# Storing half of group 10 of a linear-attention kernel in four DMAs of 96, 20, 10 and 2 partitions

One Trainium2 chip (trn2), one core. The metric is device time in microseconds (us); lower is better.

## The reference

```python
# Q, K, V: (8, 12, 512, 64) float32
Q_feat = np.maximum(0, Q) + 1
K_feat = np.maximum(0, K) + 1
KV = np.einsum('bhkd,bhkv->bhdv', K_feat, V)
K_sum = np.sum(K_feat, axis=2)
numerator = np.einsum('bhqd,bhdv->bhqv', Q_feat, KV)
denominator = np.einsum('bhqd,bhd->bhq', Q_feat, K_sum)
return (numerator / (denominator[:, :, :, None] + 1e-10)).astype(np.float32)
```

## The kernel before

The work goes through in 12 groups of 1 MB of output (`NG = 12`). The first load of K is issued by SyncE, in float32; the other loads cast to bf16 on their way and are issued by GpSimd, as are the stores of groups 0 to 9. The stores of groups 10 and 11 are issued by SyncE, each in two halves of 512 KB, so that a half can leave as soon as its multiplies on VectorE are done.

```python
    def view(t, c):
        return t.flatten_outer_dims().rearrange("(n p c) d -> p n c d", p=P, c=c)
    o_dram = view(out, C)                       # P = 128, C = 8, D = 64: 2 KB per (p, n)
    # ... cut ...
    def store(g):
        o_sb = outs.pop(g)                      # tile [128, 4, 8, 64] float32
        o_to = o_dram[:, g * NP : g * NP + NP]  # NP = 4
        if g < NG - 2:
            nc.gpsimd.dma_start(out=o_to, in_=o_sb)
            return
        for h in range(2):
            nc.sync.dma_start(out=o_to[:, h:NP:2], in_=o_sb[:, h:NP:2])
    # ... cut: features, transposes, matmuls ...
        # at the end of the program
        output(last - 1)                        # group 10
        output(last)                            # group 11
        for g in range(last - LAG, NG):         # groups 8, 9, 10, 11
            store(g)
```

A half store has 128 partitions with two runs of 2 KB each: 256 packets, 16 on each of 16 DMA engines.

Of the kernel before, what the change touches and what calls it, by code (L numbers as in the profile page):

```python
# [19 lines left out]
def kernel(  # L20
# [18 lines left out]
    nc = tc.nc  # L39

    B, H, S, D = Q.shape
    P = 128
# [3 lines left out]
    NP = 4  # L46
    NG = NPAIR // NP
# [64 lines left out]
    def store(g):  # L112
        o_sb = outs.pop(g)
        o_to = o_dram[:, g * NP : g * NP + NP]
        if g < NG - 2:
            nc.gpsimd.dma_start(out=o_to, in_=o_sb)  # L116
            return
        for h in range(2):
            nc.sync.dma_start(out=o_to[:, h:NP:2], in_=o_sb[:, h:NP:2])

    def feature(dst, src):
        nc.vector.tensor_scalar(  # L122
# [95 lines left out]
    with tc.manual_schedule():  # L218
# [15 lines left out]
        for g in range(NG - 1):  # L234
            k_features(g)
            v_blocks(g)
            q_features(g)
            if g:
                transposes(g - 1)
            if g >= 2:  # L240
                output(g - 2)
            keys_values(g)
            if g % 2 and g // 2 + 2 < NG // 2:
                load_pair(g // 2 + 2)
            if g >= LAG:
                store(g - LAG)
# [10 lines left out]
        for g in range(last - LAG, NG):  # L257
            store(g)
# [30 lines left out]
```

## Time and profile before

| | before |
|---|---|
| time, median of 3 (range) | 127.22 us (127.15 to 127.66) |
| span of the profiled run | 125.8 us |
| busy: DVE, ACT, PE, GpSimd | 70%, 54%, 52%, 22% |
| moved over the span | 400 GB/s |
| last semaphore increment of the last store | 124.87 us |

No engine of compute is near full; the DMA engines are, as the prediction shows below with the page's slices. Two more views matter. The first is the timeline of SyncE's queue (start, duration in us): its four stores.

```profile
115.35 0.38 SPq L119 DMA_DIRECT2D out_dram<-o_sb  x1
117.03 0.37 SPq L119 DMA_DIRECT2D out_dram<-o_sb  x1
118.71 0.37 SPq L119 DMA_DIRECT2D out_dram<-o_sb  x1
120.39 0.37 SPq L119 DMA_DIRECT2D out_dram<-o_sb  x1
```

The duration is the time that SyncE spends on issuing, not the transfer. The last one starts 0.03 us after the last multiply ends. The second view is the table of busy time by stretches (stretch, its length, busy time of PE, PEld, DVE, ACT, POOL with counts, granted clock, share of the 16 DMA engines, GB/s). Share and GB/s are to be read together: a low share is engines that have nothing to do, a high share with low GB/s is engines that are held up.

```profile
117.00:118.00 1.00, 0.52 (x12) 0.36 (x14) 0.93 (x5) 0.00 (x0) 0.00 (x0) 1.00 1.03 412
118.00:119.00 1.00, 0.58 (x16) 0.41 (x16) 0.96 (x3) 0.00 (x0) 0.00 (x0) 1.00 1.01 383
119.00:120.00 1.00, 0.16 (x6) 0.00 (x0) 0.97 (x3) 0.00 (x0) 0.00 (x0) 0.70 1.04 401
120.00:121.00 1.00, 0.00 (x0) 0.00 (x0) 0.36 (x1) 0.00 (x0) 0.00 (x0) 0.50 1.04 401
```

Before the change both are full: about 390 GB/s for each full share.

### The profile page before, as it was taken

What the parts mean: (1) busy time and instruction counts of PE and PEld (TensorE: products, weight loads), DVE (VectorE), ACT (ScalarE), POOL (GpSimd) and SP (SyncE); (2) the same over time, 40 slices, a digit from 0 to 9 for tenths busy, and PEclk for the clock granted to TensorE, in tenths of its full rate; (3) what the DMA queues carried; (4) which work ended last, traced back from release to release, by engine and by line L of the source; (5) the groups of instructions that cost most, each with busy time, mean ns of one, the idle gap of its engine ahead of it and who ended that gap; (6) DMA issues with size and microseconds to landing.
All of it is one profiled execution on the core that took longest, in us unless ns stands there. A gap on an engine that the chain in (4) does not pass through costs nothing.

```text
span 125.8 us, 2337 instructions
## 1 busy us (share of the span) xinstructions
PE 65.2 (52%) x960; PEld 48.4 (39%) x960; DVE 88.2 (70%) x188; ACT 68.0 (54%) x87; POOL 27.8 (22%) x43
## 2 busy tenths in 40 slices
PE   0005939000059784796918476006978569694500
PEld 0003627000036564574806365004656447472300
DVE  4896280206199799999989990629959999758920
ACT  7832296006700889629892962750087971987000
POOL 6990213000002082023700260212221002020000
PEclk9999999755555999689999999955589976999955
DMA  3999999999999999999999999999999999999991
GB/s 76 341 211 209 210 213 211 210 212 211 212 211 212 211 214 212 210 212 214 253 414 287 209 210 212 213 369 380 209 210 210 211 287 418 418 417 410 403 391 72
DMA packets 13419, 32.13 MB, mean 255 GB/s; under 512 B 608, under 2 KB 608, under 8 KB 13408
## 3 DMA queue, kind: packets, MB, share of 16 engines
q0 software_dynamic: 12048, 28.84, 98.3%
q1 hardware_dynamic: 1360, 3.15, 6.8%
q8 instruction: 7, 0.11, 0.3%
q14 instruction: 4, 0.03, 0.1%
HBM read 37.75 MB, written 12.58 MB: 400 GB/s over the span
## 4 chain that ended last, share of the span: by engine, by line
DMA 40%; DVE 26%; PE 18%; POOL 6%; issue 6%; DVEq 0%; POOLq 0%
DMA q_raw<-in_Q_dram 40%; DVE o_sb L200 15%; PE kva_ps L157 11%; DVE v_all L140 4%; PE qt_ps L176 3%; DVE recip L199 3%; PE o_ps L189 3%; POOL v_raw L99 2%; DVE qf L122 2%; DVE kf L122 2%; POOL q_raw L99 1%; POOL kva_diag L231 1%; POOL k_raw L99 1%; POOL identity masks.py:199 0%; POOL identity masks.py:197 0%
## 5 line engine op out<-in xcount | busy, mean ns | idle before, releaser
L157 PE MATMUL kva_ps<-v_all,kf 128*64 128x320 bf16 x384 | 36.4, 356 | 13.1 <-DVE v_all L140 13.1
L189 PE MATMUL o_ps<-kva_diag,qt 128*64 128x130 bf16 x384 | 19.1, 234 | 40.9 <-DVE o_sb L200 40.4
L200 DVE TENSOR_TENSOR o_sb<-o_ps,recip 128x512 f32<-128x512 f32 x48 | 33.2, 692 | 1.6
L140 DVE COPY v_all<-v_raw 32x2048 bf16<-32x2048 bf16 x36 | 26.5, 736 | 10.9 <-DMA v_raw<-in_V_dram 10.6
L157 PEld LDWEIGHTS <-kf 128*64 128x64 bf16 x384 | 25.3, 133 | 20.9 <-DVE v_all L140 13.3
L189 PEld LDWEIGHTS <-qt 128*64 128x64 bf16 x384 | 12.7, 114 | 46.4 <-DVE o_sb L200 44.6
L138 ACT COPY v_all<-v_raw 32x2048 bf16<-32x2048 bf16 x12 | 22.7, 1894 | 13.3 <-DMA v_raw<-in_V_dram 13.1
L177 ACT COPY qt<-qt_ps 128x1024 bf16<-128x1024 bf16 x24 | 29.7, 1308 | 0.3
L167 ACT CAST kva_diag<-kva_ps 64x256 bf16<-64x256 f32 x24 | 8.9, 371 | 33.3 <-PE kva_ps L157 33.2
L122 DVE TENSOR_SCALAR qf<-q_raw 128x1024 bf16<-128x1024 bf16 x24 | 9.1, 423 | 6.6 <-DMA q_raw<-in_Q_dram 6.5
L99 POOL DMA_DIRECT2D k_raw<-in_K_dram x7 | 5.3, 754 | 38.1 <-DVE kf L122 37.3
L116 POOL DMA_DIRECT2D out_dram<-o_sb x10 | 8.4, 846 | 22.6 <-DVE o_sb L200 16.4
L176 PE MATMUL qt_ps<-identity,qf 128*128 128x128 bf16 x192 | 13.1, 222 | 0.0
L199 DVE RECIPROCAL recip<-o_ps 128x8 f32<-128x8 f32 x48 | 9.6, 199 | 4.9 <-PE o_ps L189 4.8
L122 DVE TENSOR_SCALAR kf<-k_raw 128x1024 bf16<-128x1024 bf16 x22 | 8.7, 437 | 6.0 <-DMA k_raw<-in_K_dram 6.0
L176 PEld LDWEIGHTS <-qf 128*128 128x128 bf16 x192 | 11.0, 99 | 3.3 <-issue 3.0
L99 POOL DMA_DIRECT2D v_raw<-in_V_dram x8 | 6.1, 764 | 18.8 <-ACT v_all L138 10.7
L99 POOL DMA_DIRECT2D q_raw<-in_Q_dram x8 | 5.9, 741 | 4.2 <-DMA q_raw<-in_Q_dram 4.2
L213 DVE MEMSET v_all<- 128x3072 f32 (+1 forms) x2 | 4.4, 2192 | 1.1 <-DVE ones L225 0.7
L168 ACT CAST kva_diag<-kva_ps 64x4 bf16<-64x4 f32 x24 | 4.0, 169 | 0.0
L214 ACT COPY v_all<-zero 128x2048 f32<-128x2048 f32 x2 | 3.7, 1894 | 0.0
L214 ACT ACT_TABLE_LOAD x1 | 1.3, 1283 | 0.7 <-PEq L273 0.7
(12 smaller groups left out, 4.6 us busy)
## 6 DMA issues: line engine op xcount, KB each, us to landing
out_dram<-o_sb POOLq DMA_DIRECT2D x10, 1024.0 KB, 20.2
k_raw<-in_K_dram POOLq DMA_DIRECT2D x4, 1024.0 KB, 18.0
v_raw<-in_V_dram POOLq DMA_DIRECT2D x4, 1024.0 KB, 20.9
q_raw<-in_Q_dram POOLq DMA_DIRECT2D x4, 1024.0 KB, 25.0
v_raw<-in_V_dram POOLq DMA_DIRECT2D x4, 512.0 KB, 17.3
q_raw<-in_Q_dram POOLq DMA_DIRECT2D x4, 512.0 KB, 17.1
out_dram<-o_sb SPq DMA_DIRECT2D x4, 512.0 KB, 5.1
k_raw<-in_K_dram POOLq DMA_DIRECT2D x3, 512.0 KB, 23.3
```

Source lines behind the costliest of these rows:

```text
L99: nc.gpsimd.dma_start(out=t[:, ms], in_=drams[x][:, 2 * groups[0] : 2 * groups[-1] + 2])
L116: nc.gpsimd.dma_start(out=o_to, in_=o_sb)
L122: nc.vector.tensor_scalar(out=dst, in0=src, scalar1=1.0, scalar2=1.0, op0=ALU.add, op1=ALU.max)
L138: nc.scalar.copy(out=v_blk[g % 2][ps, b], in_=v_raw[ps])
L140: nc.vector.tensor_copy(out=v_blk[g % 2][ps, b], in_=v_raw[ps])
L157: nc.tensor.matmul(kva_ps[64 * n : 64 * n + 64], lhsT=kf[:, c, n, :], rhs=vb[:, :, n, c, :], start=(c == 0), stop=(c == C2 - 1),)
L167: nc.scalar.copy(out=kva[ps, :, n, 0:D], in_=kva_ps[ps, sb : sb + 4, :])
L176: nc.tensor.transpose(qt_ps[:, c, :], qf[:, half * C + c, :, :], identity)
L177: nc.scalar.copy(out=qt[:, :, :, half], in_=qt_ps)
L189: nc.tensor.matmul(ops[c // 4][64 * j : 64 * j + 64, c // 2 % 2, (c % 2) * W : (c % 2) * W + W], lhsT=qt[:, c, 32 * b : 32 * b + 32, :], r ...
L199: nc.vector.reciprocal(out=recip, in_=cells[:, :, :, :, D:D1])
L200: nc.vector.tensor_tensor(out=o_sb[:, h:NP:2, 4 * i : 4 * i + 4].rearrange("p n (b c) d -> p b c n d", b=2), in0=cells[:, :, :, :, 0:D], i ...
```

## The change

The DMA engines end one after another; some are late. By the section of the Trainium skill that the prediction cites first, a DMA from SyncE whose partitions don't divide by 16 runs on fewer engines, the lower-numbered ones. So the change cuts one half store in four, to move work from engines 10 to 15 to engines 0 to 9.

```diff
         for h in range(2):
-            nc.sync.dma_start(out=o_to[:, h:NP:2], in_=o_sb[:, h:NP:2])
+            parts = (0, 96, 116, 126, P) if (g, h) == (NG - 2, 0) else (0, P)
+            for lo, hi in zip(parts, parts[1:]):
+                nc.sync.dma_start(out=o_to[lo:hi, h:NP:2], in_=o_sb[lo:hi, h:NP:2])
```

## The prediction

> **What bounds the kernel now.** I read the page first: the slices, then the part on DMA issues, then the queue's own waits, and last the table by stretches of the end.
>
> ```profile
> DMA  3999999999999999999999999999999999999991
> GB/s 76 341 211 209 210 213 211 210 212 211 212 211 212 211 214 212 210 212 214 253 414 287 209 210 212 213 369 380 209 210 210 211 287 418 418 417 410 403 391 72
> ...
> out_dram<-o_sb POOLq DMA_DIRECT2D x10, 1024.0 KB, 20.2
> ...
> out_dram<-o_sb SPq DMA_DIRECT2D x4, 512.0 KB, 5.1
> ```
>
> The DMA engines are busy in every slice but the first and the last: the kernel is bound by its transfers from end to end. From the thirty-fourth slice on only stores run, at 391 to 418 GB/s until the last slice. The chain on the page ends in the last DVE multiply, but what ends the span is the landing of what that multiply released. The waits of SyncE's queue say so:
>
> ```profile
> SPq L119 <- DVE recip L199: 117.1, 3, 114.3
> SPq L284 <- DMA out_dram<-o_sb: 3.7, 3, 1.2
> ```
>
> Line 284 is the end of the program. Its 3.7 us in three waits are waits for the four stores of line 119 that SyncE issues, each 512 KB: group 10 half 0, group 10 half 1, group 11 half 0, group 11 half 1. The timeline of SyncE has them at 115.35, 117.03, 118.71 and 120.39 us, 0.37 us of issuing each and 1.68 us apart. The last multiply ends at 120.36, the span at 125.8. What moves between shows in the table of stretches (the last two columns are the mean share of the 16 DMA engines and GB/s):
>
> ```profile
> 120.50:121.00 0.50, 0.00 (x0) 0.00 (x0) 0.00 (x0) 0.00 (x0) 0.00 (x0) 0.50 1.02 393
> ...
> 122.00:122.50 0.50, 0.00 (x0) 0.00 (x0) 0.00 (x0) 0.00 (x0) 0.00 (x0) 0.50 1.03 401
> 122.50:123.00 0.50, 0.00 (x0) 0.00 (x0) 0.00 (x0) 0.00 (x0) 0.00 (x0) 0.50 0.78 303
> 123.00:123.50 0.50, 0.00 (x0) 0.00 (x0) 0.00 (x0) 0.00 (x0) 0.00 (x0) 0.50 0.43 164
> 123.50:124.00 0.50, 0.00 (x0) 0.00 (x0) 0.00 (x0) 0.00 (x0) 0.00 (x0) 0.50 0.17 66
> 124.00:124.50 0.50, 0.00 (x0) 0.00 (x0) 0.00 (x0) 0.00 (x0) 0.00 (x0) 0.50 0.06 25
> ```
>
> Up to 122.5 all engines work. Then the share goes 0.78, 0.43, 0.17, 0.06 (0.06 is one engine of 16): the engines run dry one after another, and the last works alone. If they ended together, the 0.5 x (0.78 + 0.43 + 0.17 + 0.06) = 0.72 us of full work left at 122.5 would be done by 123.2, and not at 124.5. So the most that any evening out of the engines can give is 1.3 us, one per cent of the time.
>
> The trace's record of the last store's semaphore gives this engine by engine. Its sixteen increments come at 122.98 us and, after that, at +0.02, 0.05, 0.07, 0.09, 0.16, 0.38, 0.54, 0.57, 0.60, 0.84, 0.88, 0.92, 1.31, 1.32 and 1.88 us, so the last at 124.87. Six stand apart, at +0.84 and later: ten engines are early and six late. From that last increment to the end of the span are 0.9 us of closing waits and drains, which the change leaves.
>
> The lag is older than this store: it is 2.3 to 2.5 us between the first and the last increment of every DMA from 90 us to 121 us, hardly growing while stores alone run. All engines then have the same work at the same rate; what was lost before is carried along, as no queue runs dry. Its origin can be seen early. In the DMA that landed first at 22.7 us the spread is 0.38 us. Next an instruction fetch of 16 KB starts at 23.1, and the DMA after it has fifteen increments within 0.35 us and one at 1.53.
>
> **What the Trainium skill says.** (1) The page DMA: Bandwidth & Descriptors, section Why a DMA increments its semaphore by 16 and not by 1: a DMA runs on the largest k of at most 16 engines that divides the slowest dimension of both sides, and from SyncE these are the lowest-numbered k. Hence 128 and 96 partitions take 16 engines, 20 and 10 take ten, 2 takes two. The trace agrees for 128 (sixteen spread increments per store); for the others nothing has run yet. (2) The same page, Latency and other measured facts: engines 7 and 15 are "usually slower" in traces. The trace here does not number the engines; it agrees that some are late, with one 0.56 us behind the rest. (3) Runtime: NRT & Kernel Launch, Instruction fetch mechanics: instruction memory is refilled in blocks of 16 KiB by DMA. The trace has seven such packets on the queue for instructions, and at least the one at 23.1 us left one engine 1.2 us late. (4) SBUF — State Buffer, Door 1: partitions 0 to 63 lie behind eight ports and 64 to 127 behind the other eight, so that a part of the partitions need not reach all sixteen. No row of the trace tests that; it feeds a rival below.
>
> **The change part by part.** It removes one store of 128 partitions and adds four of 96, 20, 10 and 2: the same bytes, so the sum of the work is unchanged.
> - Issue: four times 0.37 us is 1.49 us, from 115.35 to 116.84 with nothing between. The next store's data is there at 117.03, so 0.19 us is left for three gaps. Even a store issued 0.3 us late does no harm: the queued stores keep the engines busy (share 1.02 until 122.5).
> - Data: a partition has two runs of 2 KB, two packets. Before, each engine has 128/16 x 2 = 16. After: all engines get 96/16 x 2 = 12; the lowest ten get 2 x 2 = 4 more from the 20, and 1 x 2 = 2 from the 10; the lowest two get 2 from the last. That is 20 packets on engines 0 and 1, 18 on engines 2 to 9, 12 on engines 10 to 15 (40 + 144 + 72 = 256, as before).
> - A packet's time: the last packets of the trace, of the one engine still working, start at 123.976, 124.056, 124.136 and so on to 124.456 us, 80 ns apart. The 4 KB packets of the full stage start 155 to 156 ns apart on an engine, almost the same per byte. So an engine alone is no faster than one of sixteen, and an engine's end is its own count of packets times 80 ns. Engines 10 to 15 gain 4 x 80 = 0.32 us, engines 2 to 9 lose 0.16 us, engines 0 and 1 lose 0.32 us.
> - Completion packets: two or three more on the ten engines, 9 ns each: 0.02 to 0.03 us, none on the six.
> - The end: if the six late engines are the numbers 10 to 15, which the cut of ten to six fits, the last increment goes from +1.88 to +1.56, the next from +1.32 to +1.00; the early ten go at worst from +0.60 to +0.95. The slowest still decides, and all of its 0.32 us reach the end. If the second latest is among the ten, it goes to +1.50 and still does not decide. The early ones have slack besides: the records have the earliest engines dry for some 0.3 us before their part of the last store arrives.
> - Closing waits: three semaphores more, of DMAs long landed; each such wait took under 0.1 us and comes before the last. Nothing.
> Sum: 127.22 - 0.32 + 0 = 126.90 us.
>
> **The rivals.** (A) The late engine is not among 10 to 15. Engine 7 is one of the two that the skill names. Then the end goes up 0.16 us, or 0.32 if it is 0 or 1: 127.4 to 127.6 us. For it: no view here numbers the engines, and a fetch may fall to another engine in another execution. Against it: ten and six are just the split of the increments. (B) Ports: 96 partitions in runs of six put ten engines onto the even ports and six onto the odd ones, and the remainder then all reads behind odd ports. The engines that we want faster could wait. Against it: six engines have eight ports, and older stores are mixed in. If it takes half the gain: 127.05 us. (C) Issue: a store on fewer engines may take longer to issue than 0.37 us, or the four may wait on one another's landing (some 4.5 to 5 us from issue). The first costs nothing up to about a microsecond, because the late engine still has the older packets to do; the second would hold back the last store and give 129 us or more. The four write disjoint rows and read one tile, so I see no reason for it: 2%. (D) Nothing measurable: the three runs before span 127.15 to 127.66, 0.5 us, more than the effect.
>
> **Range and chances.** I give the step with 10 to 15 late seven or eight chances in ten (-0.32, or about half of it under B), and A two (+0.16 to +0.32). Weighted, that is about -0.2; the most likely is -0.3. I say 126.95 us. With the scatter of the runs, 0.2 us either way around either outcome, 126.55 to 127.45. Two per cent are 2.5 us: faster by that is impossible when evening out can give 1.3 us at most, so 0.01; slower needs C's second form, 0.01.
>
> **What would show it.** In the profile of the changed kernel: seven stores of line 119 on SyncE, the first four within 1.6 us from about 115.4; the last increment of the last store some 0.3 us earlier, with the sixteen spread by about 1.6 us and not 1.88; the share in the stretches after 122.5 higher at first and then gone by about 124.2; DVE, ACT and PE as before. An end at the old place or later with the latest increment at +2.0 or more would prove A; packets of over 100 ns in the first store's time on the late engine B; a late fourth store C.

## The result, and the profile after

The changed kernel takes 128.75 us in the median of 6 runs (128.43 to 129.48), the kernel before 127.38 beside it (127.15 to 127.98). The ratio is 1.011, with a 95% interval of 1.0069 to 1.0151. Ratios here are the mean time of one kernel's fast runs over that of the other's fast runs of the same rounds, so not quite the ratio of the medians quoted. It is 1.1% slower, within the two per cent of "same", but 1.8 us above the 126.95 predicted and outside the range.

The page's slices after the change:

```profile
DMA  3999999999999999999999999999999999999892
GB/s 89 331 212 208 212 210 212 210 208 212 212 211 213 212 215 210 211 213 215 274 417 259 207 213 211 221 400 343 212 210 213 210 337 423 417 413 413 265 368 107
```

In the place of 403 there is a slice at 265 GB/s. The table by stretches shows it in finer steps:

```profile
117.00:118.00 1.00, 0.58 (x12) 0.35 (x8) 0.97 (x3) 0.00 (x0) 0.00 (x0) 0.81 1.04 360
118.00:119.00 1.00, 0.12 (x4) 0.00 (x0) 0.97 (x3) 0.00 (x0) 0.00 (x0) 0.50 0.97 258
119.00:120.00 1.00, 0.00 (x0) 0.00 (x0) 0.15 (x1) 0.00 (x0) 0.00 (x0) 0.50 0.66 184
120.00:121.00 1.00, 0.00 (x0) 0.00 (x0) 0.00 (x0) 0.00 (x0) 0.00 (x0) 0.50 0.98 373
```

Both kinds of loss are there. From 118 to 119 the engines are busy (0.97) and move 258 GB/s, two thirds of what that share moved before: they are held up. From 119 to 120 the share falls to 0.66 as well: some have nothing to do. The timeline of SyncE's queue tells where the second comes from:

```profile
114.14 0.35 SPq L121 DMA_DIRECT2D out_dram<-o_sb  x1
114.54 1.34 SPq L121 DMA_DIRECT2D out_dram<-o_sb  x1
115.92 2.22 SPq L121 DMA_DIRECT2D out_dram<-o_sb  x1
118.18 0.26 SPq L121 DMA_DIRECT2D out_dram<-o_sb  x1
118.49 0.42 SPq L121 DMA_DIRECT2D out_dram<-o_sb  x1
118.96 2.01 SPq L121 DMA_DIRECT2D out_dram<-o_sb  x1
121.01 0.47 SPq L121 DMA_DIRECT2D out_dram<-o_sb  x1
```

The stores of 20 and 10 partitions took 1.34 and 2.22 us to issue, and a later one of 128 took 2.01. The last store was issued at 121.01 us, 1.86 us after its data was ready (the last multiply ended at 119.15; in this run the data came early), but only 0.62 us later than before (120.39).

The end, in half-microseconds, and the queue's last waits:

```profile
122.50:123.00 0.50, 0.00 (x0) 0.00 (x0) 0.00 (x0) 0.00 (x0) 0.00 (x0) 0.50 1.00 389
123.00:123.50 0.50, 0.00 (x0) 0.00 (x0) 0.00 (x0) 0.00 (x0) 0.00 (x0) 0.50 1.01 397
123.50:124.00 0.50, 0.00 (x0) 0.00 (x0) 0.00 (x0) 0.00 (x0) 0.00 (x0) 0.50 1.00 381
124.00:124.50 0.50, 0.00 (x0) 0.00 (x0) 0.00 (x0) 0.00 (x0) 0.00 (x0) 0.50 0.63 229
124.50:125.00 0.50, 0.00 (x0) 0.00 (x0) 0.00 (x0) 0.00 (x0) 0.00 (x0) 0.50 0.12 45
125.00:125.50 0.50, 0.00 (x0) 0.00 (x0) 0.00 (x0) 0.00 (x0) 0.00 (x0) 0.50 0.05 20
```

```profile
SPq L286 <- DMA out_dram<-o_sb: 3.6, 3, 1.2
```

All engines now work to 124.0 us and not to 122.5, and one still works alone at 125. The last increment of the last store is at 125.75, not 124.87. Fourteen of the sixteen come within 0.21 us, the other two at +0.69 and +1.19. So the engines do end closer together, only because the early ones have become late.

**The latest engine can be followed from store to store** in the trace's semaphore records, which the packed trace holds and no view prints. Its last increments are 121.42 us (the store of 96), 121.74 (of 20; four packets later), 121.93 (of 10; two packets), 123.21, 124.49 and 125.75 (sixteen packets each, 1.26 to 1.28 us). It was never idle in this time, so the late issue did not touch it. And it takes part in the stores of 20 and 10 but not in that of 2 (landed by 119.85), so it is one of engines 2 to 9: the change gave it work. But its packets in the half store are 18 in the place of 16, some 0.16 us (an estimate, two packets of 80 ns), of the 0.88 us by which the last increment moved. Most of the rest is there before these stores land. Group 9, the last store that GpSimd issued, landed last at 120.61 us, 0.80 us later than before (119.81). That is 4.1 us after the last increment of group 8 (116.51); before, it was 2.5 (117.31). In the records of packets between 116 and 121.5 us, 13 of GpSimd's 4 KB packets, nearly all of group 9, took over 230 ns, up to 798; before, one did (444). Their usual time is 160.

Not all of the 4.1 us need be collisions. An engine can have packets of both queues under way: in after_again, below, the store of 96 had landed on all engines by 120.91 us, before the last of group 9 (121.53). And in ident2 the same stretch takes 3.4 us with one long packet. One profile doesn't settle the cause; the runs below are there for that.

### The profile page after: what moved, and what is told of

Its sections match the earlier page's. It is cut to its first block, busy times and chain, and to the rows that moved or that the text cites. A ratio compares the mean times of both kernels' runs of the same rounds, so it can differ in the third digit from the quotient of the medians.

```text
span 126.7 us, 2342 instructions
## 1 busy us (share of the span) xinstructions
PE 67.8 (53%) x960; PEld 50.4 (40%) x960; DVE 88.1 (70%) x188; ACT 68.0 (54%) x87; POOL 27.9 (22%) x43
## 4 chain that ended last, share of the span: by engine, by line
DMA 52%; DVE 21%; PE 12%; issue 6%; POOL 3%; POOLq 0%; DVEq 0%
DMA q_raw<-in_Q_dram 43%; DVE o_sb L202 12%; DMA v_raw<-in_V_dram 9%; PE kva_ps L159 7%; DVE v_all L142 4%; DVE recip L201 2%; PE qt_ps L178 2%; PE o_ps L191 2%; POOL v_raw L99 2%; DVE qf L124 2%; DVE kf L124 1%; POOL q_raw L99 1%; POOL k_raw L99 0%; POOL zero L221 0%; POOLq L99 0%
## 5 line engine op out<-in xcount | busy, mean ns | idle before, releaser
L159 PE MATMUL kva_ps<-v_all,kf 128*64 128x320 bf16 x384 | 38.7, 371 | 12.6 <-DVE v_all L142 10.7
L191 PE MATMUL o_ps<-kva_diag,qt 128*64 128x130 bf16 x384 | 19.6, 238 | 37.7 <-DVE o_sb L202 37.2
L159 PEld LDWEIGHTS <-kf 128*64 128x64 bf16 x384 | 27.2, 138 | 20.4 <-DVE v_all L142 12.4
```

Of the source, the lines that this page charges most:

```text
L159: nc.tensor.matmul(kva_ps[64 * n : 64 * n + 64], lhsT=kf[:, c, n, :], rhs=vb[:, :, n, c, :], start=(c == 0), stop=(c == C2 - 1),)
L191: nc.tensor.matmul(ops[c // 4][64 * j : 64 * j + 64, c // 2 % 2, (c % 2) * W : (c % 2) * W + W], lhsT=qt[:, c, 32 * b : 32 * b + 32, :], r ...
```

## The experiments

Three theories, from the trace. **Ports**: several engines reading neighbouring partitions collide, in the new stores and with the older store still under way. **Issue**: stores in direct succession hold up SyncE, so later ones come late. **Skew**: the work went to the engine that was latest. The ports in the expectations are those of the page that the prediction cites for its rival B. Each edit below is to the kernel before; (10, 0) is the half store that the change cuts. "Long" counts packets from 116 to 121.5 us: 2 KB packets of the SyncE stores, and of ScalarE's where it issues some, over 150 ns (usual: 84), and 4 KB packets of GpSimd's over 230 ns (usual: 160).

| run | stores in place of (10, 0) | ratio (95% interval) | long 2 KB | long 4 KB |
|---|---|---|---|---|
| before | 128 | | 1 | 1 |
| after | 96, 20, 10, 2 | 1.011 (1.0069 to 1.0151) | 33 | 13 |
| after_again | the same | 1.0101 (1.0059 to 1.0144) | 12 | 19 |
| p96_32 | 96, 32 | 1.0082 (1.0053 to 1.0111) | 35 | 10 |
| p96_32_again | 96, 32 | 1.0096 (1.0067 to 1.0126) | 29 | 14 |
| p4x32 | 4 x 32 neighbours | 1.0093 (1.0063 to 1.0122) | 43 | 16 |
| act_small | 96; 20, 10, 2 from ScalarE | 1.0062 (1.0027 to 1.0097) | 47 | 10 |
| n2x128 | 128, 128 (2 KB each) | 1.001 (0.9989 to 1.0031) | 0 | 2 |
| s4x32 | 4 x 32, a step apart | 1.0023 (0.9984 to 1.0061) | 1 | 2 |
| s64_32_32 | 64, 32, 32, a step apart | 1.0002 (0.9972 to 1.0032) | 0 | 2 |
| s_even4 | 64, 32, 16, 16, a step apart | 1.0021 (0.9991 to 1.0051) | 0 | 2 |
| s_skew4 | 64, 32, 20, 12, a step apart | 1.0019 (0.9987 to 1.0051) | 7 | 3 |

Every run of this table with neighbouring partitions has ten or more long 4 KB packets and is slower; none of the others has over three, and none of these is clearly slower. Five more runs with five or six stores carried a cost of their own and come below.

The profiles allow one more check. Executions bring different lags into the end, so take the time from the last increment of group 7 to that of the last store: 10.06 us before and 10.08 to 10.38 in the five runs without neighbours, but 10.91 to 11.73 in five of the six with them. The sixth, after_again, has 10.29: its one profile doesn't show the loss in this stretch.

### Two stores of all partitions (n2x128)

```diff
-            nc.sync.dma_start(out=o_to[:, h:NP:2], in_=o_sb[:, h:NP:2])
+            rows = (h, h + 2) if (g, h) == (NG - 2, 0) else (h,)
+            for n in rows:      # one row block per store for (10, 0), else both in one
+                ns = slice(n, n + 1) if len(rows) == 2 else slice(h, NP, 2)
+                nc.sync.dma_start(out=o_to[:, ns], in_=o_sb[:, ns])
```

> The half of group 10 as two stores of all 128 partitions, one row block each, issued back to back; every engine keeps its 16 packets and its own port. Three theories for the 1.1% lost. Ports (the parts of few partitions make several engines read behind the same SBUF ports, packets of 300 ns and more): no collision here, so time as before, ratio 0.998 to 1.003, no 2 KB packets over 150 ns to speak of. Issue (stores that follow one another at once stall SyncE's issue by 1.3 to 2.2 us, so later stores come late): the second store's issue takes over 1 us, and the ratio is somewhere over 1.003. Skew (work was moved onto an engine that was already the latest): no skew, as before.

Ratio 1.001. The second store, of all 128 partitions, took 1.18 us to issue, the third 1.21, the fourth 0.72; the last was issued on time. So the wait in issuing is not a matter of 20 or 10 partitions: it befalls a store that follows another at once. And it costs nothing here that can be seen: the share of the DMA engines stays at 1.02 or more from 117 to 122 us.

### Four stores of neighbours, and four a step apart (p4x32, s4x32)

```diff
+            parts = (0, 32, 64, 96, P) if (g, h) == (NG - 2, 0) else (0, P)   # p4x32
+            for lo, hi in zip(parts, parts[1:]):
+                nc.sync.dma_start(out=o_to[lo:hi, h:NP:2], in_=o_sb[lo:hi, h:NP:2])
```
```diff
+            step = 4 if (g, h) == (NG - 2, 0) else 1                          # s4x32
+            for lo in range(step):
+                nc.sync.dma_start(out=o_to[lo:P:step, h:NP:2], in_=o_sb[lo:P:step, h:NP:2])
```

> The half of group 10 as four stores of 32 neighbouring partitions each: the same number of stores as in the change, each on 16 engines, every engine 16 packets as before. Ports: 32 neighbours lie behind half of the ports, so packets of 150 to 600 ns between 116 and 121 us and a ratio of 1.01 or more. Issue: stalls of over 1 us in issuing, whatever the ports. Skew: no skew, so ratio 1.000. If there are stalls in issuing and no long packets, the issue theory; if long packets and no stalls, ports.

> The same four stores of 32 partitions, but each takes every fourth partition, so that one store is spread over all 16 ports. Issue count, engines per store and packets per engine are those of the run with neighbouring partitions. Ports: far fewer long packets than there, ratio 0.998 to 1.004. Issue: the same stalls as there, the same time as there. Skew: 1.000.

Ratios 1.0093 and 1.0023; all timed runs of the first (128.08 to 128.82 us) are above all of the second (127.04 to 127.88). Number of stores, engines per store and packets per engine are the same in both. The stretch from 118 to 119 us, first with neighbours, then a step apart:

```profile
118.00:119.00 1.00, 0.00 (x0) 0.00 (x0) 0.70 (x2) 0.00 (x0) 0.00 (x0) 0.50 1.02 313
```

```profile
118.00:119.00 1.00, 0.58 (x14) 0.42 (x16) 0.93 (x4) 0.00 (x0) 0.00 (x0) 1.00 0.62 236
```

The stepped stores move less in this stretch, and yet the kernel is faster. With neighbours a full share moves 307 GB/s: engines are held up and, as the later end says, the latest among them. A step apart a full share moves 381, as before; engines are idle, but they are the early ones. That is the lesson of the pair: idle time of the early engines costs nothing until they fall behind the latest. One thing was not held equal: the waits in issuing reached 2.09 us with neighbours and 1.27 a step apart. But the last store was issued at 120.25 us with neighbours and at 120.48 a step apart, so late issue does not make the difference.

### 96 and 32 (p96_32, p96_32_again)

```diff
+            parts = (0, 96, P) if (g, h) == (NG - 2, 0) else (0, P)
+            for lo, hi in zip(parts, parts[1:]):
+                nc.sync.dma_start(out=o_to[lo:hi, h:NP:2], in_=o_sb[lo:hi, h:NP:2])
```

> The half of group 10 as two stores, of 96 and 32 partitions, both on 16 engines: 12 and 4 packets each, no skew, but the 96 as in the change. Ports: long packets as in the change, ratio 1.005 to 1.012. Issue: if the stall follows the store of 96, the 32 takes 1.3 us to issue as the 20 did; if it comes from stores on ten engines, 0.4 us. Skew: 1.000.

> Collisions without skew, two stores: 1.007 to 1.010 as before. What the change has above that is skew and the issue of two more stores.

Ratios 1.0082 and 1.0096, without any skew: nearly all of the change's loss. The store of 32, on 16 engines, took 1.31 us to issue, as the 20 did, so stores on ten engines are not the cause. In the first profile the last store was issued 1.80 us after its data, in the second 0.03 us: the loss is the same, so late issue of the last store isn't it. By the clock of the span it left at 120.67 and 120.20 us, against 120.39 before the change. Issue waits of the later whole stores reached 3.17 and 2.20 us here, over the 1.46 us that no store of SyncE passed in the runs a step apart. That collisions lengthen them is likely, but not shown.

### The small stores from ScalarE (act_small)

```diff
+            parts = (0, 96, 116, 126, P) if (g, h) == (NG - 2, 0) else (0, P)
+            for lo, hi in zip(parts, parts[1:]):
+                eng = nc.scalar if lo else nc.sync
+                eng.dma_start(out=o_to[lo:hi, h:NP:2], in_=o_sb[lo:hi, h:NP:2])
```

> The change with the stores of 20, 10 and 2 partitions issued by ScalarE, which is idle then; SyncE has its four stores and the spacing of before. Ports: nothing changes, ratio 1.007 to 1.011, long packets as in the change. Issue: SyncE stalls less, its last store is issued less than 0.5 us after its data is ready, and if that bound the change the ratio falls to 1.003 or less.

Ratio 1.0062, between the two forecasts. SyncE's last store was issued 0.03 us after its data, and the long packets stayed (47 and 10). Most of the loss remains without late issue. Whether the rest was saved by issuing can't be said: the interval overlaps the change's.

### The change again (after_again)

> The change once more, for a ratio on the same chip as the next two: 1.008 to 1.013. In its profile, as in the first one, the latest engine should appear among the ten increments of the store of 20 if the lateness of one of the engines 0 to 9 is the rule, and be missing there if it differs from execution to execution.

Ratio 1.0101. The last increment was at 125.53 us. One of the two engines that ended last took part in the store of 10, but they ended within 0.04 us of each other, so which was latest is not sure.

### Even and skewed, four stores a step apart (s64_32_32, s_even4, s_skew4)

```diff
+            # s64_32_32: [(0,128,2), (1,128,4), (3,128,4)]
+            # s_even4:   [(0,128,2), (1,128,4), (3,67,4), (67,128,4)]
+            # s_skew4:   [(0,128,2), (1,128,4), (3,83,4), (83,128,4)]
+            cuts = CUTS if (g, h) == (NG - 2, 0) else [(0, P, 1)]
+            for lo, hi, step in cuts:
+                ps = slice(lo, hi, step)
+                nc.sync.dma_start(out=o_to[ps, h:NP:2], in_=o_sb[ps, h:NP:2])
```

> The same with 64, 32 and 32 partitions a fixed step apart, all on 16 engines, 16 packets on each: the run to compare the skew with. Ports: ratio 0.998 to 1.004, as with four times 32 a step apart. Issue: stalls of 1.0 to 1.3 us for the second and third store; harmless as long as the last store is issued less than 1 us late.

> 64, 32, 16 and 16 partitions a step apart, all on 16 engines: four stores as in the change, hardly any collisions, no skew, no coming round of the semaphores. Issue alone: if the late issue of four stores counts, 1.003 or more; if the idle time of the early engines covers it, 0.999 to 1.002.

> 64, 32, 20 and 12 partitions a step apart: 18 packets on engines 0 to 9, 14 on 10 and 11, 12 on 12 to 15; otherwise as the even run. Skew alone: above the even run by 0.001 to 0.002 if the latest engine is usually among the lower ones, below it by 0.001 to 0.002 if it is among the upper ones. If it comes out 0.005 or more above, the skew is more than its packets.

Ratios 1.0002, 1.0021 and 1.0019. Issue waits were there in each (1.1 to 1.4 us, two to four times). The even run of four stores by stretches:

```profile
118.00:119.00 1.00, 0.35 (x8) 0.16 (x8) 0.96 (x3) 0.00 (x0) 0.00 (x0) 0.58 0.78 305
119.00:120.00 1.00, 0.00 (x0) 0.00 (x0) 0.54 (x1) 0.00 (x0) 0.00 (x0) 0.50 0.50 193
120.00:121.00 1.00, 0.00 (x0) 0.00 (x0) 0.00 (x0) 0.00 (x0) 0.00 (x0) 0.50 0.81 311
```

It moved about as little as the change in these stretches (809 against 815 GB/s summed), at 387 GB/s per full share (the change: 312): idle, not held up. Its ratio is 1.0021, with an interval that includes 1. So late issue (here 0.89 us after the data, for the last store) is worth 0.2% by itself, if anything, and at most 0.5%. The skew adds or takes nothing that can be seen (1.0019 against 1.0021). In this, too, the forecast was a choice of two small effects, and neither is resolved.

### Five and six stores, and a cost of their own (s_skew, s5_even, s_skew_act, ident, ident2)

```diff
+            # s_skew:  64, 32 | 20, 10, 2     ident:  64, 32 | 15, 8, 7, 2
+            # s5_even: 32, 32, 32 | 16, 16    ident2: 64, 32 | 10, 9, 8, 5
+            # all a step of 2 or 4 apart, from SyncE; s_skew_act: as s_skew, the last three from ScalarE
```

> The counts of packets per engine are those of the change (20 on engines 0 and 1, 18 on 2 to 9, 12 on 10 to 15), but every store takes partitions a fixed step apart, so that it is spread over the ports: 64 (every second), 32 (every fourth), then 20, 10 and 2 of the last quarter. Ports: without the collisions of the change, ratio 0.998 to 1.005, few packets over 150 ns. Skew onto the latest engine: against the same run without skew the end is 0.16 us later if the latest engine is among 0 to 9, 0.3 us earlier if it is among 10 to 15. Issue: six more stores back to back take 1.2 to 1.3 us each, so the last store is issued over 2 us late and the ratio is 1.01 or more, if that is what binds.

> Five stores (32, 32, 32, 16, 16 partitions, four apart), all on 16 engines, 16 packets on each: five issues back to back as in the run with skew over five stores (1.0087), but no skew and hardly any collisions. Issue: 1.005 to 1.010, all sixteen increments of the last store within 0.4 us, its issue over 1 us after its data; then the late issue alone accounts for that run. Skew: 1.000 to 1.002, and the 0.9% of that run were the uneven counts.

> The skew alone: 64 and 32 partitions a step apart from SyncE, and 20, 10 and 2 from ScalarE, so that neither ports nor late issues should matter (issue of the last store within 0.6 us of its data). Counts per engine as in the change. If the latest engine is among 10 to 15, ratio 0.997 to 0.999; if it is among 2 to 9, 1.000 to 1.002 with the end 0.16 us later; the 1.1% of the change is not in the skew in either case.

> To learn which engines are late: 64 and 32 partitions a step apart on all engines, then 15 (engines 0 to 14), 8 (0 to 7), 7 (0 to 6) and 2 (0 and 1). If the latest engine is number 7, a late increment appears in the store of 8 and not in that of 7; if it is 15, it is missing from the store of 15. Time is not what it is for; 128 us or more, by late issues.

> Which engine is latest: the last quarter as stores of 10, 9, 8 and 5 partitions (engines 0 to 9, 0 to 8, 0 to 7, 0 to 4). In the run with 15, 8 and 7 the latest engine was one of 8 to 14, in the changed kernel one of 2 to 9; if it is always the same, it is 8 or 9: late in the store of 10, and in that of 9 only if it is 8, and not in that of 8. If it differs from execution to execution, any other pattern. Time 128 to 129 us by late issues.

Ratios 1.0087 (1.0059 to 1.0115), 1.0068 (1.0037 to 1.0099) and 1.0067 (1.004 to 1.0095); the two single looks took 128.65 and 128.35 us. Few or no long packets: 0 to 6 and 0 to 2. At first this looked like a case for skew or issue. But their profiles have a tail that the others lack. The closing waits of SyncE's queue, first for s64_32_32, then for s_skew:

```profile
SPq L287 <- DMA out_dram<-o_sb: 3.6, 3, 1.2
```

```profile
SPq L287 <- DMA out_dram<-o_sb: 3.6, 1, 3.6
```

One wait in the place of three. With the load at the start, these kernels have nine or more DMAs from SyncE and ScalarE together, and the eight semaphores for them come round: the last store gets one that has been used, and the closing waits, which go through the semaphores in order, have it first. After it lands, seven more waits of 0.06 us follow: the span ends 1.34 us after the last increment, not 0.91. These 0.43 us are 0.34% of the time; less that, the three ratios would be about 1.005, 1.003 and 1.003. This sum is an estimate. What is left, 0.3 to 0.5%, long packets don't explain, and it stays undivided: s5_even has no skew, and s_skew_act has its last store issued on time (0.03 us). The forecast for s_skew_act, 1.002 at most, failed. In s_skew all engines ended within 0.20 us, so there the late issue (1.12 us) can have reached the end.

**Which engine is latest.** By the Trainium skill's page DMA: Bandwidth & Descriptors, section Why a DMA increments its semaphore by 16 and not by 1, a DMA on k engines from SyncE takes the lowest-numbered k, and the increments of the others are written at once. The trace agrees as far as it goes: the changed kernel's store of 20 has one early record at 116.00 us, ahead of its data, and then ten. So a store on k engines shows whether the latest engine is among the lowest k: its increment follows the one of the store before by its packets' time (some 0.2 us for two packets). In ident, all late increments reappear in the store of 15, so engine 15 was not late; the latest, 120.61 us there, does not reappear in the store of 8, so it was one of 8 to 14. In ident2, the latest reappears in the stores of 10, 9 and 8 (120.90, 121.10, 121.31 us), not in that of 5, so it was one of 5 to 7. In the changed kernel it was one of 2 to 9. It is not the same engine in these three profiles, so no fixed cut relieves it every time.

### SBUF side or HBM side (x_sb_step, x_hbm_step)

Both give a wrong result: the rows of the half group land permuted.

```diff
+                for i in range(4):
+                    near, far = slice(32 * i, 32 * i + 32), slice(i, P, 4)
+                    # x_sb_step:  out=o_to[near, h:NP:2], in_=o_sb[far, h:NP:2]
+                    # x_hbm_step: out=o_to[far, h:NP:2],  in_=o_sb[near, h:NP:2]
```

> Wrong result on purpose (rows of half a group land permuted). Four stores of 32: read from every fourth partition of SBUF, written to 32 neighbouring places of HBM. If the collisions are on the SBUF side: few long packets, ratio 0.999 to 1.004. If they are on the HBM side: long packets and 1.007 or more.

> Wrong result on purpose. Four stores of 32: read from 32 neighbouring partitions of SBUF, written to every fourth place of HBM. SBUF side: long packets (over 230 ns for some ten of the 4 KB packets of group 9) and 1.007 or more. HBM side: few, and 0.999 to 1.004.

The medians on the same chip were 127.25 us (127.05 to 127.38) with SBUF stepped and 128.00 (127.55 to 128.32) with SBUF neighbours: no overlap. Long 2 KB packets: 1 against 70. The stretch from 120 to 121 us, first with SBUF stepped, then with SBUF neighbours:

```profile
120.00:121.00 1.00, 0.00 (x0) 0.00 (x0) 0.40 (x1) 0.00 (x0) 0.00 (x0) 0.50 1.04 391
```

```profile
120.00:121.00 1.00, 0.00 (x0) 0.00 (x0) 0.01 (x1) 0.00 (x0) 0.00 (x0) 0.50 0.95 281
```

A full share moves 376 GB/s in the one and 296 in the other. So the collisions of the 2 KB packets are on the SBUF side. That what they share there is a port of the skill's map, and not something else of neighbouring partitions, no run tells. The ratios to the kernel before were 0.9958 (0.9921 to 0.9994) and 1.0015 (0.9974 to 1.0057); the kernel before scattered more than usual there (127.22 to 128.28), and I take no gain from the first. One thing was not as expected: only 5 long 4 KB packets with SBUF neighbours, against 16 when the HBM rows were neighbours too, and a ratio below the 1.007 expected. Whether the HBM side has a share in holding up group 9 stays open.

## Why the prediction was wrong

- **The bound** was right: only transfers set the end, and the latest engine's last packets ended the span.
- **The data step failed.** It said that "an engine's end is its own count of packets times 80 ns", taken from an engine alone and from engines that each served a share of all 128 partitions. Both are cases without collisions: before the change, one 2 KB packet in the window took over 150 ns. Reading neighbours, 12 to 47 of them did in the runs of the table, up to 474 in the changed kernel, and GpSimd's 4 KB packets took up to 798. This is the term that was mis-sized. Rival B named it, but allowed it only to halve a gain of 0.32 us; the 96 and 32 alone, without skew, cost 0.8 to 1.0% (1.0 to 1.2 us). So the range had no room for it. The argument against B, that "older stores are mixed in", was upside down: the older store's packets were among those held up.
- **The issue step failed too**: 0.37 us was read from stores 1.68 us apart. In direct succession the second took 1.18 to 1.46 us in all the kernels that had one on SyncE. Rival C's first form was true, beyond the microsecond that I allowed it. Its cost, taken alone, was still small (1.0021, not clear of 1), for the reason given there: the early engines have slack. They were not even busy throughout before: "up to 122.5 all engines work" passes over the stretch from 121.0 to 121.5 us, with a share of 0.89. C's second form, stores waiting on one another's landing, is not seen: the store of 20 was issued by 115.88 us, before any packet of the 96 had moved (the first at 116.95).
- **The choice of engines failed.** "Ten and six are just the split of the increments" was numerology: the counts fitted, and no view numbered the engines. Rival A was right in the profiled run of the change, though its sign, a latest increment at +2.0 us or more, did not come (+1.19): the early engines had become late too. But the skew's own worth, as s_skew4 against s_even4 shows, is below what these runs resolve.
- **No semaphore cost** was right for the seven stores of the change: the span still ended 0.92 us after the last increment. One store more would have made nine DMAs, and it would have been wrong by 0.43 us.
- **The chances** of two per cent either way were sound: the whole matter is 1.4 us.

How the 1.0 to 1.1% divides: collisions 0.8 to 1.0%, by the runs of 96 and 32; what is left, 0.3% at most, is within the intervals and stays undivided between skew and issue. No kernel here beats the one before with a correct result.

## What to carry to other kernels

A store cut by ranges of partitions is not just a smaller store: here its engines read neighbouring partitions, held up one another and an older store, and the second store in a row cost 1.18 to 1.46 us of issue. If a store has to be cut, cut it along the free dimension (1.001 here), or take partitions a step apart (1.000 to 1.002 with three or four stores), and check that the latest engine, not the average, gains. A time per packet or per issue read from well-spaced, full transfers is no price for small ones in a row.

## What the Trainium skill lacked or had wrong

- SBUF — State Buffer, section Door 1: that a range of 32 partitions reaches half of the ports fits the runs (long 2 KB packets: 43 with 32 neighbours, 1 with every fourth partition), though no run shows the ports themselves. It has no figure for what other DMAs in flight pay: 4 KB packets of another queue's store went from 160 to as much as 798 ns.
- DMA: Bandwidth & Descriptors, section Issuing engines are not separate DMA queues, calls the time to initiate a DMA "usually small relative to the DMA itself". A store issued right behind another took SyncE 1.18 to 1.46 us, and up to 3.17 beside collisions, against 0.37 alone; I found this on no page.
- The same page, Latency and other measured facts: engines 7 and 15 are usually slower. Here the latest was one of 2 to 9, of 8 to 14 and of 5 to 7 in three profiles: neither 7 nor 15 in the second, and 7 is possible in the others.
- Runtime: NRT & Kernel Launch, Instruction fetch mechanics: crossing a block is "mostly hidden". It doesn't say what the fetch costs other DMAs. The 16 KB packet at 23.1 us took 1.01 us; the DMA after it had one engine some 1.2 us late (spread 1.53 us, 0.38 in the DMA before), and a spread of about 1.5 us or more stayed until the end of the kernel. That the fetch is the cause is inferred from the order of the two.
- No page has the cost of closing waits when DMA semaphores come round: 0.43 us here.
